# RWKV tiles: three factors moved into constants of small matrix products

## The chip, the cores and the metric

The kernel runs on one core of a Trainium2 chip. The metric is the device time of one execution, in microseconds (us). The kernel before took 769.58 us (median of three runs, 769.44 to 770.28). TensorE is written PE, VectorE DVE, ScalarE ACT, GpSimd POOL and the engine that issues most transfers SP.

## The reference, cut to what matters

One decoder layer: a norm and one input projection, then two groups of heads side by side (an RWKV-7 time mixing with 8 heads of 64, and a sparse attention), one output projection, and a gated feed-forward part. SEQ is 512 and D_MODEL 1024. The change touches the end of the RWKV group, where `y` is the result of the recurrence:

```python
    mean = jnp.mean(y, axis=-1, keepdims=True)
    var = jnp.mean(jnp.square(y - mean), axis=-1, keepdims=True)
    y = ((y - mean) * lax.rsqrt(var + LNX_EPS)).reshape(B, S, R_WIDTH) * lnx_w + lnx_b
    bonus = jnp.sum(rh * kh * r_k.astype(f32), axis=-1, keepdims=True) * vh
    y = (y + bonus.reshape(B, S, R_WIDTH)) * g
```

The recurrence is linear in `v`, so a `v` whose mean over each head's 64 channels has been taken away gives a `y` whose mean is zero; the kernel centres `v` and never centres `y`.

## The kernel before, in words

The program is written with a tile framework: a planner orders each engine's instructions at compile time by the program's order and by what is ready, and every buffer belongs to a tag with a fixed number of slots. A tile of a tag gets its slot at its first write, and waits for the release of an earlier tile when all slots are taken. So work of different parts runs interleaved on every engine.

The RWKV part keeps its tensors with channels on the partitions: `rar`, `rk_`, `rb`, `rv` are [128, 4, 512], where 128 partitions hold two heads (64 channels each), 4 is the pair of heads, and 512 the tokens. It works in four tiles of 128 tokens, each in three stages, in the order `stage_a(t)`, `stage_c(t-1)`, `stage_b(t)`, `bonus(t)`, with a `stage_c(3)` at the end:

- `stage_a` (L772) builds the tile's chunk matrices. L784 makes products of keys and queries, L787 masks them on DVE. Then four tensors are transposed to tokens on the partitions, four transposes each (L798). The second of them is `v`: DVE sums each head's 64 channels out of PSUM (L804) and two instructions, one for each half of the partitions, subtract the mean while they copy (L806). L813, L818, L826, L832, L838 and L843 are the products that follow.
- `stage_b` (L850) carries the state over the tile's two chunks (L862, L864, L865, L866).
- `bonus` (L876): four DVE instructions multiply r, the column `r_k` and k (L880), one product of 512 columns with `ones2` sums each head and spreads the sum over its channels (L882), DVE multiplies with `v` (L883), POOL adds `lnx_b` (L884).
- `stage_c` (L886): ACT squares `y` (L891), four products with 32 columns of `ones2` sum each head (L895), ACT copies the sums out (L896), a transpose puts tokens on the partitions (L897), DVE computes the inverse root in eleven small instructions (L899 and `rsqrt`, L449), ACT copies it 64 times for each head (L902), four transposes bring it back to channels (L904), and DVE multiplies it in (L906), multiplies by the weight `lnx_w` (L907), adds the bonus (L908) and multiplies by the gate (L909).

Beside these tiles PE, DVE, ACT and POOL run the attention (from L917 on: L980 and L981 scores, L986 to L990 softmax, L993 transposes of the probabilities, L1001 products with v, L965 and L969 the compressed branch). Before the tiles a triangular system is solved on DVE and POOL (`solve2`, L541, instructions L556 and L557; then `solve4`, L561). After them come the output projection and the feed-forward part (L163 to L165).

PSUM tag `rb` has one buffer, which `stage_b`, `bonus` and `stage_c` use in program order; `ra` has two, which `stage_a` uses. SBUF tag `t4` has four slots, which, among others, `cm` (constants and results of the compressed branch), `blk` and `inv` (the solve), `az` and `qt2` (the tiles), `gain2` (L1007) and three buffers of the feed-forward part's first weights (`t1`, `t3` and `t2`, loaded at L1123 and L1125, and written by DVE at L1141) take in turn. Tag `rp` has one slot, used in `compressed` (L684).

A product of two float32 operands is two MATMUL instructions in the trace; a transpose is one.

Of the kernel before, what the change touches and what calls it, by code (L numbers as in the profile page):

```python
# [12 lines left out]
AF = mybir.ActivationFunctionType  # L13
OP = mybir.AluOpType
AX = mybir.AxisListType
# [9 lines left out]
EPS, LNX_EPS = 1e-6, 64e-5  # L25
# [21 lines left out]
def hybrid_layer(ctx: ExitStack, tc: tile.TileContext, x, positions, norm_mix, w_in, mu_shift, w0, w2, a0, a2,  # L47
                 g2, k_k, k_a, r_k, lnx_w, lnx_b, pe_k, wk1, bk1, wk2, pe_v, wv1, bv1, wv2, w_out, norm_ffn,
                 w_gate, w_up, w_down, norm_final, out):
    nc = tc.nc  # L50
    PE, DVE, ACT, POOL = nc.tensor, nc.vector, nc.scalar, nc.gpsimd
# [6 lines left out]
    def ps(tag, shape=(128, 512), dtype=F32):  # L58
        return pp.tile(list(shape), dtype, name="ps_" + tag, tag=tag, bufs=PS_BUFS[tag])
# [3 lines left out]
    def st(shape, tag, bufs=1, dtype=F32):  # L63
        return sb.tile(list(shape), dtype, name=tag, tag=tag, bufs=SB_BUFS.get(tag, bufs))
# [17 lines left out]
    ident = st([128, 128], "ident")  # L82
# [38 lines left out]
    for g in range(2):  # L121
        nc.sync.dma_start(posci[g * 32:g * 32 + 31], bass.AP(tensor=positions.tensor, offset=positions.offset + 31,
                                                               ap=[[16, 31], [1, 1]]))
# [129 lines left out]
    ones2 = st([128, 128], "ones2")  # L253
# [9 lines left out]
    for c in range(2):  # L263
        h = amask[c * 64:(c + 1) * 64]
# [5 lines left out]
    for q in range(4):  # L270
        h = amaskd[32 * q:32 * q + 32]
# [38 lines left out]
    def col(name, i):  # L310
        return cs[:, row0[name] + i:row0[name] + i + 1]
# [57 lines left out]
    for a in range(2):  # L369
        p = ps("s", (128, 2, 256))  # L370
# [78 lines left out]
    def rsqrt(o, x):  # L449

        y, b = (st([128, 16], "rs", 3)[:, 0:x.shape[1]] for _ in range(2))
        DVE.tensor_scalar(b.bitcast(I32), x.bitcast(I32), 1, None, op0=OP.logical_shift_right)
        DVE.tensor_scalar(y.bitcast(I32), b.bitcast(I32), -1.0, 1597463007.0, op0=OP.mult, op1=OP.add)
        for n in range(3):
            DVE.tensor_mul(b, x, y)
            DVE.scalar_tensor_tensor(b, b, -0.5, y, op0=OP.mult, op1=OP.mult)
            DVE.scalar_tensor_tensor(o if n == 2 else y, b, 1.5, y, op0=OP.add, op1=OP.mult)
# [301 lines left out]
    uv = yuv[:, 1024:2048].rearrange("p (c h n) -> p c h n", c=2, h=8)  # L759
# [7 lines left out]
    pg = T["pg"]  # L767
    POOL.memset(ybd, 0.0)

    PQ = [(i, par, 2 * i + par, slice(par * 64, par * 64 + 64)) for i in range(4) for par in range(2)]  # L770

    def stage_a(t):  # L772
# [22 lines left out]
        for n, src in enumerate((rar[:, :, 0, tl], rv[:, :, tl], rb[:, :, tl], sk)):  # L795
            p = ps("ra", (128, 4, 128))
            for i in range(4):
                PE.transpose(p[:, i], src[:, i], ident)  # L798
            pv = p.rearrange("p i (q d) -> p (i q) d", q=2)
            if n == 0:  # L800
                ACT.activation(az[:, :, 0:64], pv, AF.Copy)
            elif n == 1:
                vs = st([128, 8], "vs", 2)
                DVE.tensor_reduce(vs, pv, axis=AX.X, op=OP.add)  # L804
                for c, cr, co in HALF:
                    DVE.scalar_tensor_tensor(uv[co, c], vs[cr, :, None].to_broadcast([64, 8, 64]), -1.0 / 64, pv[cr], op0=OP.mult, op1=OP.add)  # L806
            else:
                for c, cr, co in HALF:
                    ACT.activation(bk[cr if n == 2 else co, c], pv[cr], AF.Copy)
# [60 lines left out]
    def cb(name):  # L870
        return cs[:, row0[name]:row0[name] + 4, None].to_broadcast([128, 4, 128])

    def bonus_of(t):
        return abc[:, t, 4:8].rearrange("p h a s -> p h (a s)")

    def bonus(t):  # L876
        tl = slice(t * 128, t * 128 + 128)
        tmp = bonus_of(t)
        for i in range(4):
            DVE.scalar_tensor_tensor(tmp[:, i], rar[:, i, 1, tl], col("r_k", i), rk_[:, i, tl], op0=OP.mult, op1=OP.mult)  # L880
        p = ps("rb", (128, 4, 128))
        PE.matmul(p, ones2, tmp, start=True, stop=True)  # L882
        DVE.tensor_mul(tmp, p, rv[:, :, tl])  # L883
        POOL.tensor_add(tmp, tmp, cb("lnx_b"))  # L884

    def stage_c(t):  # L886

        tl = slice(t * 128, t * 128 + 128)
        ys = rar[:, :, 0, tl]
        tmp = abc[:, t, 0:4].rearrange("p h a s -> p h (a s)")  # L890
        ACT.activation(tmp, ys, AF.Square)  # L891

        p = ps("rb", (128, 2, 128))
        for i in range(4):
            PE.matmul(p[32 * i:32 * i + 32, 0], ones2[:, 48:80], tmp[:, i], start=True, stop=True)  # L895
        ACT.activation(tmp[:, 0], p[:, 0], AF.Copy)  # L896
        PE.transpose(p[:, 1], tmp[:, 0], ident)  # L897
        rn = st([128, 16], "rn", 2)[:, 0:8]
        DVE.tensor_scalar(rn, p[:, 1, 0:128:16], 1.0 / 64, LNX_EPS, op0=OP.mult, op1=OP.add)  # L899
        rsqrt(rn, rn)  # L900
        p = ps("rb", (128, 4, 128))
        ACT.activation(tmp.rearrange("p i (q d) -> p (i q) d", q=2), rn[:, :, None].to_broadcast([128, 8, 64]), AF.Copy)  # L902
        for i in range(4):
            PE.transpose(p[:, i], tmp[:, i], ident)  # L904
        yc = ys
        DVE.tensor_mul(yc, ys, p)  # L906
        DVE.tensor_mul(yc, yc, cb("lnx_w"))  # L907
        DVE.tensor_add(yc, yc, bonus_of(t))  # L908
        DVE.tensor_mul(yc, yc, gate_[:, :, tl])  # L909

# [352 lines left out]
```

## Time and profile before

| | |
|---|---|
| profiled execution | 770.73 us |
| its span (first to last instruction) | 769.0 us |
| mean granted TensorE clock | 0.984 of 2.4 GHz |
| PE busy | 738.6 us (96%), 6093 instructions |
| DVE busy | 543.3 us (71%), 1052 |
| ACT busy | 381.5 us (50%), 652 |
| POOL busy | 160.0 us (21%), 258 |
| chain of waits, by engine | PE 74%, DVE 15%, DMA 6% |

Busy time is the share of the span in which at least one instruction of the engine runs. Matmuls are pipelined, so one that lasts 270 ns may be followed 110 ns later by the next; what a run of them costs is read from the chain of waits, which gives each piece the time up to the next piece. The tiles run from about 213 to 350 us after the start of the span.

### The profile page before, as it was taken

How to read it: one execution, taken by the hardware profiler on the slowest of the kernel's cores; microseconds unless marked ns; L12 is line 12 of the kernel's file. 1: busy time of each engine (PE TensorE's matmuls, PEld its weight loads, DVE VectorE, ACT ScalarE, POOL GpSimd, SP SyncE). 2: the span in 40 equal slices, each digit the busy share in tenths (PEclk: the TensorE clock that was granted, in tenths of full speed). 3: DMA queues.
4: the chain of work that ended last, by engine and by line, in shares of the span. 5: the costliest groups of instructions: out<-in, count | busy, mean ns of one | idle time of the engine just before them, and what ended most of it. 6: DMA issues, size and time to landing. Idle time of an engine off the chain costs nothing.

```text
span 769.0 us, 14989 instructions
## 1 busy us (share of the span) xinstructions
PE 738.6 (96%) x6093; PEld 648.1 (84%) x6093; DVE 543.3 (71%) x1052; ACT 381.5 (50%) x652; POOL 160.0 (21%) x258
## 2 busy tenths in 40 slices
PE   8999999998889999999996899999999999999996
PEld 7867888898877878867786899999999998888885
DVE  5488689789768987875659497888695994333235
ACT  7398643224277776676447344444443552233224
POOL 3210054058345542442001102020202000000000
PEclk9999999999989999999998999999999999999998
DMA  7722543100051000321218569696768444322102
GB/s 247 223 82 84 164 110 110 55 2 2 3 219 30 3 1 3 85 83 56 83 55 192 110 176 203 161 223 151 161 159 221 112 153 147 110 68 97 55 1 110
DMA packets 69243, 82.83 MB, mean 108 GB/s; under 512 B 4868, under 2 KB 62806, under 8 KB 69174
## 3 DMA queue, kind: packets, MB, share of 16 engines
q1 hardware_dynamic: 57558, 70.34, 28.5%
q0 software_dynamic: 11616, 11.54, 9.9%
q8 instruction: 48, 0.79, 0.4%
q14 instruction: 21, 0.17, 0.1%
HBM read 79.77 MB, written 2.10 MB: 106 GB/s over the span
## 4 chain that ended last, share of the span: by engine, by line
PE 74%; DVE 15%; DMA 6%; issue 2%; ACT 1%; POOL 0%; SPq 0%; DVEq 0%; POOLq 0%; ACTq 0%
PE ps_ra L165 7%; PE ps_ra L164 7%; PE ps_ra L163 6%; PE ps_pj L165 6%; PE ps_pj L163 6%; PE ps_pj L164 6%; PE ps_s L165 4%; PE ps_s L163 4%; PE ps_s L164 4%; PE ps_o L1001 3%; DVE wlo L146 3%; PE ps_pj L993 2%; DMA L<-in_w_up_dram 2%; DMA wraw<-in_w_up_dram 2%; DMA L<-in_w_gate_dram 2%
## 5 line engine op out<-in xcount | busy, mean ns | idle before, releaser
L144 ACT ACTIVATE whi<-wraw 128x1024 fp32r<-128x1024 f32 (+1 forms) x79 | 78.5, 1033 | 33.2 <-PE ps_s L165 8.2
L146 DVE TENSOR_TENSOR wlo<-wraw,whi 128x1024 fp32r<-128x1024 f32 (+1 forms) x62 | 77.7, 1284 | 14.9 <-ACT whi L144 11.3
L146 DVE TENSOR_TENSOR L<-b,L 128x512 fp32r<-128x512 f32 x24 | 16.2, 691 | 57.1 <-PE ps_rb L164 55.1
L990 POOL TENSOR_SCALAR whi<-whi,m,gates 128x128 f32<-128x128 f32 (+3 forms) x64 | 42.5, 679 | 36.9 <-DVE m L988 28.7
L144 ACT ACTIVATE L<-b 128x512 fp32r<-128x512 f32 x24 | 14.9, 632 | 70.0 <-PE ps_rb L164 65.1
L164 PE MATMUL ps_ra<-wlo,L 128*128 128x256 f32 (+1 forms) x140 | 47.6, 340 | 0.2 <-DVE wlo L146 0.2
L163 PE MATMUL ps_ra<-whi,L 128*128 128x256 f32 (+1 forms) x140 | 47.4, 340 | 0.2 <-ACT L L144 0.2
L165 PE MATMUL ps_ra<-whi,L 128*128 128x256 f32 (+1 forms) x140 | 47.0, 337 | 0.0
L165 PE MATMUL ps_pj<-whi,L 128*128 128x256 f32 (+1 forms) x140 | 46.3, 332 | 0.0
L164 PE MATMUL ps_pj<-wlo,L 128*128 128x256 f32 (+1 forms) x140 | 46.3, 331 | 0.0
L163 PE MATMUL ps_pj<-whi,L 128*128 128x256 f32 (+1 forms) x140 | 45.9, 332 | 0.0
L164 PE MATMUL ps_ra<-L,whi 128*128 128x256 f32 (+2 forms) x128 | 44.3, 346 | 1.0 <-DVE L L146 1.0
L163 PE MATMUL ps_ra<-L,whi 128*128 128x256 f32 (+2 forms) x128 | 44.1, 345 | 0.9 <-ACT L L144 0.9
L165 PE MATMUL ps_ra<-L,wlo 128*128 128x512 f32 (+2 forms) x120 | 41.2, 343 | 0.0
L987 ACT ACTIVATE whi<-whi,m 128x128 f32<-128x128 f32 (+3 forms) x64 | 35.4, 554 | 9.3 <-DVE m L986 8.1
L165 PE MATMUL ps_pj<-L,wlo 128*128 128x512 f32 (+1 forms) x112 | 38.8, 346 | 0.1
L163 PE MATMUL ps_pj<-L,whi 128*128 128x512 f32 (+1 forms) x104 | 36.3, 349 | 0.2 <-ACT whi L144 0.2
L164 PE MATMUL ps_pj<-L,whi 128*128 128x512 f32 (+1 forms) x104 | 35.9, 346 | 0.0
L986 DVE CUSTOM_DVE_ANT_0 whi<-ps_s,negb 128x128 f32<-128x128 f32 (+3 forms) x64 | 29.3, 484 | 5.9 <-PE ps_pj L993 2.5
L1137 POOL DMA_DIRECT2D t<-in_w_up_dram x6 | 7.9, 1322 | 115.1 <-DVE whi L146 50.4
L163 PEld LDWEIGHTS ps_ra<-whi,L 128*128 128x128 f32 x140 | 27.6, 197 | 3.1 <-ACT L L144 0.6
L164 PEld LDWEIGHTS ps_ra<-wlo,L 128*128 128x128 f32 x140 | 27.5, 196 | 3.0 <-DVE wlo L146 0.5
(627 smaller groups left out, 2462.4 us busy)
## 6 DMA issues: line engine op xcount, KB each, us to landing
wraw<-in_w_gate_dram SPq DMA_DIRECT2D x22, 512.0 KB
wraw<-in_w_down_dram SPq DMA_DIRECT2D x11, 1024.0 KB
wraw<-in_w_in_dram SPq DMA_DIRECT2D x9, 1024.0 KB
t<-in_w_up_dram POOLq DMA_DIRECT2D x12, 512.0 KB, 7.4
wraw<-in_w_up_dram SPq DMA_DIRECT2D x11, 512.0 KB
L<-in_w_up_dram POOLq DMA_DIRECT2D x10, 512.0 KB, 8.9
wraw<-in_w_out_dram SPq DMA_DIRECT2D x4, 1024.0 KB
wraw<-in_w_in_dram SPq DMA_DIRECT2D x6, 512.0 KB
```

Source lines behind the costliest of these rows:

```text
L144: ACT.activation(hi, src, AF.Copy)
L146: (POOL if pool else DVE).tensor_sub(lo, src, hi.bitcast(F32))
L163: PE.matmul(o, lh, rh, start=start, stop=False)
L164: PE.matmul(o, lh, rl, start=False, stop=False)
L165: PE.matmul(o, ll, rh, start=False, stop=stop)
L986: DVE.tensor_tensor_reduce(pr[:, i], pS[:, i], negb[:, S - n:S], scale=-1.0, scalar=3e38, op0=OP.add, op1=OP.min, accum_out=m[:, i, 0:1])
L987: ACT.activation(pr[:, i], pr[:, i], AF.Exp, scale=-1.0, bias=m[:, i, 0:1], accum_out=m[:, i, 1:2])
L990: POOL.tensor_scalar(pr[:, i], pr[:, i], m[:, i, 2:3], gv[:, 1 + b0 + i, h:h + 1], op0=OP.mult, op1=OP.mult)
L993: PE.transpose(pT[:, j], prr[:, x, j * 128:j * 128 + 128], ident)
L1001: PE.matmul(po[q, 2 * g:2 * g + 2], vtok[:, j % (t + 1), b0 + j // (t + 1), g], pTs[:, par, j], start=False, stop=g == 1 and bs[-1] == 1 a ...
L1137: POOL.dma_start(t1, quarter(w_up, 0), accum_op=OP.add)
```

## The change

Constants are built once before the tiles. `onesr` is `ones2` scaled by the column `r_k`, one 128x128 block for each pair of heads (four POOL instructions). `lnxh` is the weight `lnx_w`, laid out as 8 rows (heads) by 4 blocks of 128 channels, loaded by one small transfer to 8 partitions and cut to each head's own 64 channels by two POOL selects. `heads` has a one where a channel belongs to a head. `centre` is the identity minus 1/64 in each head's block (one DVE instruction). `onesr` and `lnxh` live in a tile of tag `t4`, `heads` and `centre` in one of tag `rp`, both until the last tile.

In each tile, `v` is multiplied by `centre` in place of its transposes, so it arrives transposed and centred, and DVE only copies it. In `bonus` one DVE multiply over 512 columns replaces four over 128, and four products with `onesr` replace the one with `ones2`. In `stage_c` four products take the squares as the stationary operand and `heads` as 8 moving columns, and so give the sums with tokens on the partitions; the ACT copy and the transpose before the inverse root go. The inverse root (128x8) is transposed to 8x128, copied by ACT, and four products with `lnxh` spread it over the channels and apply the weight; the fourfold copy on ACT, the four transposes and DVE's multiply by `lnx_w` go.

```diff
     POOL.memset(ybd, 0.0)
 
+    con = st([128, 2, 4, 128], "t4")
+    onesr, lnxh = con[:, 0], con[0:8, 1]
+    for i in range(4):
+        POOL.tensor_scalar(onesr[:, i], ones2, col("r_k", i), None, op0=OP.mult)
+    nc.sync.dma_start(lnxh, bass.AP(tensor=lnx_w.tensor, offset=lnx_w.offset, ap=[[0, 8], [128, 4], [1, 128]]))
+    POOL.affine_select(lnxh, lnxh, pattern=[[128, 4], [1, 128]], compare_op=OP.is_ge, fill=0.0, base=0, channel_multiplier=-64)
+    POOL.affine_select(lnxh, lnxh, pattern=[[-128, 4], [-1, 128]], compare_op=OP.is_ge, fill=0.0, base=63, channel_multiplier=64)
+    con2 = st([128, 2, 4, 32], "rp").rearrange("p a b c -> p (a b c)")
+    heads, centre = con2[:, 0:32].rearrange("p (i h) -> p i h", h=8), con2[:, 32:160]
+    POOL.memset(heads, 0.0)
+    for q in range(2):
+        v = con2[q * 64:q * 64 + 64, q:q + 1]
+        POOL.memset(bass.AP(tensor=v.tensor, offset=v.offset, ap=[list(v.ap[0]), [10, 4]]), 1.0)
+    DVE.scalar_tensor_tensor(centre, ones2, -1.0 / 64, ident, op0=OP.mult, op1=OP.add)
...
             for i in range(4):
-                PE.transpose(p[:, i], src[:, i], ident)
+                if n == 1:
+                    PE.matmul(p[:, i], src[:, i], centre, start=True, stop=True)
+                else:
+                    PE.transpose(p[:, i], src[:, i], ident)
...
             elif n == 1:
-                vs = st([128, 8], "vs", 2)
-                DVE.tensor_reduce(vs, pv, axis=AX.X, op=OP.add)
                 for c, cr, co in HALF:
-                    DVE.scalar_tensor_tensor(uv[co, c], vs[cr, :, None].to_broadcast([64, 8, 64]), -1.0 / 64, pv[cr], op0=OP.mult, op1=OP.add)
+                    DVE.tensor_copy(uv[co, c], pv[cr])
...
         tmp = bonus_of(t)
+        DVE.tensor_mul(tmp, rar[:, :, 1, tl], rk_[:, :, tl])
+        p = ps("rb", (128, 4, 128))
         for i in range(4):
-            DVE.scalar_tensor_tensor(tmp[:, i], rar[:, i, 1, tl], col("r_k", i), rk_[:, i, tl], op0=OP.mult, op1=OP.mult)
-        p = ps("rb", (128, 4, 128))
-        PE.matmul(p, ones2, tmp, start=True, stop=True)
+            PE.matmul(p[:, i], onesr[:, i], tmp[:, i], start=True, stop=True)
...
         p = ps("rb", (128, 2, 128))
         for i in range(4):
-            PE.matmul(p[32 * i:32 * i + 32, 0], ones2[:, 48:80], tmp[:, i], start=True, stop=True)
-        ACT.activation(tmp[:, 0], p[:, 0], AF.Copy)
-        PE.transpose(p[:, 1], tmp[:, 0], ident)
+            PE.matmul(p[:, 0, 0:8], tmp[:, i], heads[:, i], start=i == 0, stop=i == 3)
         rn = st([128, 16], "rn", 2)[:, 0:8]
-        DVE.tensor_scalar(rn, p[:, 1, 0:128:16], 1.0 / 64, LNX_EPS, op0=OP.mult, op1=OP.add)
+        DVE.tensor_scalar(rn, p[:, 0, 0:8], 1.0 / 64, LNX_EPS, op0=OP.mult, op1=OP.add)
         rsqrt(rn, rn)
+        PE.transpose(p[0:8, 1], rn, ident)
+        rnT = tmp[0:8, 0]
+        ACT.activation(rnT, p[0:8, 1], AF.Copy)
         p = ps("rb", (128, 4, 128))
-        ACT.activation(tmp.rearrange("p i (q d) -> p (i q) d", q=2), rn[:, :, None].to_broadcast([128, 8, 64]), AF.Copy)
         for i in range(4):
-            PE.transpose(p[:, i], tmp[:, i], ident)
+            PE.matmul(p[:, i], lnxh[:, i], rnT, start=True, stop=True)
         yc = ys
         DVE.tensor_mul(yc, ys, p)
-        DVE.tensor_mul(yc, yc, cb("lnx_w"))
```

## Rows read from the trace of the kernel before

**Rows 1.** Busy time of each engine in five stretches from the middle of the tiles to the end of the output projection (us from the span's start; in each column the busy time and the number of instructions, then PE's granted clock, the DMA engines' busy share and GB/s).

```profile
265.00:290.00 25.00, 25.00 (x302) 19.95 (x300) 21.08 (x73) 17.89 (x47) 12.37 (x20) 1.00 0.01 2
290.00:315.00 25.00, 24.77 (x342) 19.79 (x336) 20.18 (x62) 15.37 (x38) 6.86 (x10) 1.00 0.08 23
315.00:333.00 18.00, 18.00 (x237) 13.53 (x233) 15.71 (x44) 10.85 (x25) 9.01 (x9) 1.00 0.52 148
333.00:352.00 19.00, 18.11 (x126) 12.74 (x125) 15.43 (x53) 14.34 (x36) 9.97 (x12) 1.00 0.00 1
352.00:399.00 47.00, 47.00 (x227) 37.10 (x227) 25.04 (x36) 21.17 (x33) 2.26 (x3) 1.00 0.25 79
```

**Rows 2.** What PE waited for from 226 to 352 us (total us, times, longest), the largest of the five rows.

```profile
PE ps_pj L965 <- DVE t L962: 0.9, 1, 0.9
PE ps_ra L798 <- DVE whi L787: 0.2, 1, 0.2
PE ps_rb L882 <- DVE L L866: 0.2, 1, 0.2
...
```

**Rows 3.** Pieces of the chain of waits (start, us until the next piece, what): eight products of 128x128x128 in float32; then the products and transposes that the change replaces.

```profile
250.74 1.79 PE ps_ra L818 x16
...
271.29 0.86 PE ps_rb L882 x2
...
276.90 0.36 PE ps_rb L895 x8
...
279.68 0.26 PE ps_rb L897
...
344.89 0.44 PE ps_rb L904 x4
```

**Rows 4.** PE's timeline: eight products with a 128x128 float32 tile as the stationary operand and two moving columns.

```profile
130.60 1.95 PE L476 MATMUL ps_s<-ones,L 128*128 128x2 f32 x16
```

**Rows 5.** The chain of waits at the start of tile 0.

```profile
213.57 2.55 DVE L L880 x4
216.14 0.68 DVE whi L787
...
219.13 0.70 DVE whi L787
...
219.88 1.12 PE ps_ra L798 x4
```

**Rows 6.** Busy times as in rows 1, in three stretches of tile 0.

```profile
218.00:220.00 2.00, 0.72 (x8) 0.58 (x7) 1.92 (x6) 1.39 (x3) 0.19 (x1) 0.67 1.02 420
220.00:222.00 2.00, 2.00 (x13) 2.00 (x13) 1.61 (x3) 0.92 (x3) 1.26 (x2) 0.50 0.99 306
...
224.00:226.00 2.00, 2.00 (x35) 1.69 (x34) 0.00 (x0) 1.85 (x4) 1.05 (x1) 0.62 0.95 384
```

**Rows 7.** DVE's instructions of the lines that the change touches and of two that are like the new ones (duration in ns: least, median, most; then first and last start in us).

```profile
L804 DVE TENSOR_REDUCE vs<-ps_ra x4: 679/680/691, 221.0 to 301.3; 128x8 f32<-128x512 f32 x4
L806 DVE SCALAR_TENSOR_TENSOR wlo<-vs,ps_ra x8: 680/686/690, 221.8 to 303.2; 64x512 f32<-64x512 f32 x8
L880 DVE SCALAR_TENSOR_TENSOR L<-L,cs,b x16: 343/347/815, 213.6 to 292.3; 128x128 f32<-128x128 f32 x16
L907 DVE TENSOR_TENSOR L<-L,cs x4: 682/686/691, 262.0 to 347.5; 128x512 f32<-128x512 f32 x4
L908 DVE TENSOR_TENSOR L<-L x4: 684/684/965, 264.1 to 348.8; 128x512 f32<-128x512 f32 x4
L580 DVE COPY L<-ps_s x4: 678/684/689, 210.7 to 212.8; 32x512 f32<-32x512 f32 x4
```

**Rows 8.** Two steps of the solve on DVE, from its timeline (start, us, instruction).

```profile
192.69 0.35 DVE L557 TENSOR_TENSOR t<-t,smask 128x120 f32<-128x120 f32 x1
...
195.22 1.11 DVE L557 TENSOR_TENSOR t<-t,smask 128x105 f32<-128x105 f32 x1
```

**Rows 9.** The first multiply into `qt2` and the first step of the solve on POOL (the idle time before it in brackets), and the last products that read `cm`.

```profile
131.68 1.15 POOL L794 TENSOR_TENSOR t<-b,dend 128x512 f32<-128x512 f32 x1
...
161.58 1.23 POOL L556 TENSOR_TENSOR smask<-t,t 128x31 f32<-128x31 f32 x1 [28.66 <-DVE rot L239]
...
L698 PE MATMUL ps_s<-t,rp x8: 217/274/275, 160.4 to 165.2; 128*128 128x64 f32 x8
```

**Rows 10.** The loads of `t1` and `t3` on SP's queue, POOL's transfer that adds to `t3`, and the first DVE instruction that reads `t1`.

```profile
214.12 0.42 SPq L1123 DMA_DIRECT2D t<-in_w_gate_dram  x1
...
310.52 0.37 SPq L1125 DMA_DIRECT2D t<-in_w_up_dram  x1
...
315.00 1.33 POOL L1138 DMA_DIRECT2D t<-in_w_up_dram  x1 [3.83 <-DMA t<-in_w_up_dram]
...
L1141 DVE TENSOR_TENSOR t<-t,wraw x6: 1224/1226/1226, 379.5 to 610.5; 128x1024 f32<-128x1024 f32 x6
```

**Rows 11.** ACT's two instructions of `stage_c` that go.

```profile
L896 ACT ACTIVATE L<-ps_rb x4: 267/277/277, 245.2 to 334.2; 128x128 f32<-128x128 f32 x4
...
L902 ACT ACTIVATE L<-rn x4: 612/621/631, 257.1 to 342.6; 128x512 f32<-128x512 f32 x4
```

**Rows 12.** The chain of waits between tiles 2 and 3: the first and the last of a run of pieces on DVE, with the PE piece that follows it.

```profile
291.02 0.42 DVE b L846
...
298.50 0.70 DVE whi L787
...
299.34 0.63 PE ps_ra L798 x4
```

## The prediction

> **What bounds the kernel now.** I read the page's shares first: PE is busy for 96% of the span and holds 74% of the chain of waits, DVE 71% and 15%. Since the change touches only the RWKV tiles, I then read that stage by stretches [rows 1]. The reader is to see that PE is busy for 25.00 of 25, 24.77 of 25, 18.00 of 18 and 18.11 of 19 us, at full clock, and for 47.00 of 47 us in the output projection behind the tiles, while DVE is at 15.4 to 21.1 us and has room. Busy PE time is modelled, so the list of PE's waits was the check [rows 2]: from 226 to 352 us the largest wait is 0.9 us, and with the two rows left out, of 0.2 us each, all five sum to 1.7 us. PE never runs dry there because the attention fills it. So from 226 us on, a microsecond more on PE is a microsecond more in the end, and a microsecond less on DVE is worth at most its part of 1.7 us.
>
> Tile 0 is different. Its start hangs on DVE: after the solve DVE runs the four L880 of the bonus in 2.55 us, then the masks, and PE's transposes follow at 219.88 [rows 5]. PE is busy for 0.72 of 2 us before that, and its granted clock falls to half (1.2 GHz) until some way into 224 to 226 us [rows 6].
>
> **The change part by part, PE.** The price of a float32 product: sixteen instructions of L818, eight products of 128x128x128, take 1.79 us [rows 3], so an instruction is 0.112 us and four products (eight instructions) 0.90 us. Four transposes take 0.44 us (L904, the same shape as L798) [rows 3].
> - Centring: four transposes become four such products, +0.46 us. Three tiles at full clock give 1.4; in tile 0 L798 takes 1.12 us at half clock [rows 5], so I double its addition to 0.9. Together +2.3.
> - Bonus: L882's one product of 512 columns takes 0.86 us [rows 3], four of 128 columns 0.90: +0.04 a tile, +0.15.
> - Sums of the squares: L895's eight instructions take 0.36 us in all [rows 3], because each fills only 32 columns of the array. The new products load a whole 128x128 tile and move 8 columns. The nearest row is L476, the same stationary tile with 2 columns: sixteen instructions in 1.95 us, of which the last one's drain is some 0.25, so 0.11 each [rows 4]. Eight make 0.90: +0.54 a tile, +2.15. The low end is L895's own rate, +0. The transpose L897 (0.26) goes and the one of the inverse root comes, which I put at the same.
> - Spreading with the weight: four transposes of 0.44 become four products with 8 rows and 128 moving columns. I take 0.90, L818's, for the columns are as many: +0.46 a tile, +1.85. The low end is L895's rate, 0.36, which would be a gain of 0.1 a tile, -0.3.
>
> The sum on PE is +6.4 us, with +2.1 as the low end. The Trainium skill, "TensorE: Matmul & The Clock Gate", section "Back-to-back issue gap", puts an isolated matmul of 1 to 64 columns at a floor of about 25 ns; by that the eight instructions with 8 columns would cost 0.2 us a tile, and the sum would be 2.8 us lower. L476's rate in rows 4 speaks against it: there the load of the stationary tile sets the pace.
>
> **DVE, ACT and POOL.** A tile loses L804 (0.68), L907 (0.69) and the difference between four L880 and one multiply like L908 (about 1.14 against 0.69 at their median durations, starts overlapping); L806 becomes a copy out of PSUM of the same length, by L580 [rows 7]. That is 1.8 us a tile, 7.3 in all, and ACT loses 0.62 and 0.28 for a new copy of about 0.27 [rows 11]. From tile 1 on nearly all of it falls where PE is the bound: I take -0.3 us, from 0 to -1.7 [rows 2]. In tile 0 it is on the path: the 2.55 us of L880 (the longest took 815 ns, against 347 in the median) were run beside POOL's instructions, so the one multiply costs 0.69 undisturbed and perhaps 1.5 disturbed, by the same ratio. I take -1.1, from -0.4 to -1.9.
>
> The constants: four scalings, two selects, three clears on POOL, one small transfer, and the instruction for `centre` on DVE, about 0.35 us by L880's median. POOL stands idle for 28.66 us before the solve [rows 9], which hides its share; without that cover it would be some 3 us of POOL beside the solve. `con` is first written ahead of `qt2` in the program, so it takes the slot of `t4` that L794 took at 131.68; L794 then has to wait for `cm`, read until 165.2 [rows 9], and runs beside the solve or behind it. There a step of the solve on DVE takes 1.11 us where a longer one took 0.35 [rows 8], when POOL multiplies at the same time: +0.75. `centre` waits for the slot of `rp`, which `compressed` frees at about 170, inside the solve as well: +0.35. Together +1.1, from 0 to +1.5.
>
> The slot that `con` keeps has one more result: `t1`'s load (214.12) finds no slot and waits for `az`, as `t3`'s does now (310.52). Nobody reads it before 379.5 us [rows 10], so I cost the delay at nothing. But POOL's transfers that add to `t1` and `t3` wait in POOL's queue for these loads (3.83 us for `t3`), and behind them stand L990, L961 and L884, for which PE's attention products wait. The one that comes new into 310 to 335 us costs between 0 and 3.8; I take 0, since PE had other work while POOL stood in the first.
>
> **The sum.** 6.4 - 1.1 - 0.3 + 1.1 = +6.1 us. The profiled execution took 770.73 us (span 769.0 and 1.7 around it), and would take 776.8; it lies 1.15 above the median of 769.58, from which I forecast 775.7. The ends: all lows give -1.5 (2.1 - 1.9 - 1.7, the constants at nothing), all highs +11.3 (6.4 - 0.4 + 1.5 + 3.8).
>
> **Rivals.**
> 1. DVE ends last in the tiles, and the new products run in PE's gaps. For it: the chain of waits runs over DVE from 291.02 to 299.2 between tiles 2 and 3 [rows 12], and over L880 in tile 0. Against it: PE is busy for 24.77 of 25 us around that very stretch [rows 1]; it had other work. If true, DVE's 7.3 us less the 1.1 come off: 763.4. It decides as soon as PE's waits in the tiles are more than the added 6 us; they are 1.7. Chance 0.12.
> 2. The clock stays up in tile 0. PE's thin stretch before 219.88 gets shorter by 1.1 us or more, and the half clock around it may not come. That lasts about 6.8 us: a mean of 0.67 over two us is 1.3 us at half and the rest at full clock, 0.62 is 1.5 us, and the four us between them are taken whole [rows 6]. It costs half of this, 3.4 us, and centring's 0.46 extra: 6.1 - 3.9 = +2.2, 771.8. Against it: PE stays thin for over 3 us there whatever the bonus costs. The Trainium skill says on the same page, in Part 4 on PE-mode transpose, that transposes do not count as a busy PE for the clock; four of those in this stretch become products, which by that rule would bring the clock back sooner. No row here tells transposes and products apart in this. Chance 0.11.
> 3. POOL's transfer for `t1` holds up the attention by its whole wait: +9.9, 779.5. For it: POOL is busy for 9.97 of 19 us in the last tile [rows 1], and PE's one long wait (L965) is in a chain with POOL. Against it: PE lost nothing visible at the first such wait. Chance 0.10.
> 4. The small products are cheap (the low ends of both): +1.8, 771.4. Against it stands L476. Chance 0.05.
>
> **How the numbers follow.** The forecast, +3 to +9 us, gets 0.62. 770.5 to 780.0 holds it, rival 2, rival 3 and half of rival 4, and leaves out rival 1 and the tails. What a measurement tells from no change is about 0.2%, 1.5 us. Faster by more than that is rival 1, 0.12; within it, half of rival 4 and the low parts of rival 2 and of the forecast, 0.08; slower 0.80.
>
> **What would show it.** Right: PE busy for all but a few tenths of each stretch from 226 us to the end of the output projection, the centring products at 0.90 us for eight instructions and the sums at the same, and DVE's busy time down by some 6 to 7 us with no gain from it; `t1`'s load near 310 us. Wrong: PE's list of waits in the tiles grown by several us (then another engine or the one `rb` buffer has become the bound), the eight instructions with 8 columns in 0.4 us or less, the first transposes of tile 0 earlier by much more than 1 us, or an end of the output projection that has not moved although PE's work has grown.

## The result and the profile after

The changed kernel takes 781.19 us (median of 4 runs, 779.88 to 782.26); the ratio to the kernel before is 1.0144, with a 95% interval from 1.0124 to 1.0164, so it is about 11 us slower. Forecast were 775.7, in a range from 770.5 to 780.0. The profiled execution has a span of 780.6 us against 769.0.

Line numbers of the new kernel are higher by 14 to 18 in the tiles (L798 becomes L816 and, for `v`, L814; L818 becomes L834; L895 becomes L910; L904 becomes L919); in the solve they are the same. The first thing to read is where the 11.65 us between the two spans arise. These are starts and ends of the same instructions in both traces (us from the span's start):

| | before | after | later by |
|---|---|---|---|
| last small product before the solve (L529 ends) | 158.67 | 159.61 | 0.9 |
| POOL's first step of the solve (L556 starts) | 161.58 | 164.62 | 3.0 |
| POOL's last step (L557 ends) | 194.77 | 206.93 | 12.2 |
| DVE turns the solution (L563 starts) | 201.04 | 207.30 | 6.3 |
| the solve's products (L578 ends) | 211.63 | 221.36 | 9.7 |
| first L813, tile 0 | 224.24 | 227.17 | 2.9 |
| last L843, tile 3 | 323.32 | 328.72 | 5.4 |
| attention's last product (L1001 ends) | 367.29 | 383.01 | 15.7 |
| last transposes of the second norm (L1082 end) | 418.49 | 433.94 | 15.4 |
| last product of all (starts) | 761.76 | 773.41 | 11.65 |

Three readings. The solve, which the change does not touch, ends 6 to 12 us later. The last L843 of the tiles comes only 5.4 us later, the attention's end 15.7: in PE's queue the attention fills what the tiles leave, so whatever PE loses shows at the attention's end. And the feed-forward part gives 4 us back.

Busy times by stretch, in the columns of [rows 1], for the new kernel:

```profile
226.00:250.00 24.00, 21.07 (x311) 18.93 (x309) 12.57 (x37) 16.19 (x41) 7.79 (x13) 0.93 0.01 3
250.00:275.00 25.00, 24.00 (x357) 19.79 (x358) 19.27 (x72) 14.64 (x45) 9.42 (x20) 1.00 0.01 2
275.00:300.00 25.00, 24.27 (x330) 20.50 (x329) 18.73 (x71) 19.13 (x55) 13.05 (x22) 1.00 0.01 2
300.00:325.00 25.00, 25.00 (x318) 21.01 (x315) 21.48 (x66) 14.66 (x35) 9.27 (x12) 1.00 0.20 42
355.00:400.00 45.00, 44.75 (x237) 32.82 (x236) 24.41 (x49) 24.80 (x45) 8.39 (x11) 1.00 0.19 59
```

PE is still the bound from 250 us on, but no longer in the first tile (21.07 of 24 us, at a granted clock of 0.93). Its waits from 226 to 360 us, as in [rows 2], now sum to 5.0 us in nine rows, of which the four largest are:

```profile
PE ps_s L947 <- ACT L L948: 1.2, 1, 1.2
PE ps_ra L834 <- ACT t L830: 0.9, 1, 0.9
PE ps_ra L829 <- ACT wraw L825: 0.8, 1, 0.8
PE ps_pj L1007 <- ACT wraw L1011: 0.7, 1, 0.7
...
```

The prices of the new products, as pieces of the chain at full clock, beside [rows 3]: centring (L814), bonus (L898), sums (L910), the transpose of the inverse root (L914), spreading with the weight (L919), and the unchanged L834 as a measure.

```profile
274.15 0.89 PE ps_ra L814 x8
275.04 0.89 PE ps_rb L898 x8
283.21 1.78 PE ps_ra L834 x16
286.56 0.11 PE ps_rb L914
288.72 1.08 PE ps_rb L919 x8
310.44 0.79 PE ps_rb L910 x8
```

Centring costs 0.45 more than four transposes, the bonus 0.03 more than its one product, the sums 0.43 more than L895, the spreading 0.64 more than L904, and the transpose of the inverse root 0.15 less than L897. That is 1.40 us a tile, 5.6 in four, against 6.4 forecast, of which 0.46 was for tile 0 at half clock.

Counted from the end of the last L529, the attention ends 14.8 us later. PE's waits of 0.2 us and more up to there sum to 13.2 us against 9.4 before, and 6.8 us more at half clock (13.6 against 6.8) are worth up to 3.4; with the products these make 12.8, and 2 us are left without a row. So the larger part of the 14.8 is not the products, and begins ahead of the tiles. POOL's queue at the start of the solve (start, us, instruction, idle time before it in brackets), and one line from further on:

```profile
164.51 0.15 POOL L711 MEMSET rot<- 128x64 f32 x1 [22.07 <-DVE kct L240]
164.62 0.24 POOL L556 TENSOR_TENSOR smask<-t,t 128x31 f32<-128x31 f32 x1
164.81 1.65 POOL L776 TENSOR_SCALAR_AFFINE_SELECT t<-t 8x512 f32<-8x512 f32 x1
166.44 0.27 POOL L557 TENSOR_TENSOR t<-t,smask 128x31 f32<-128x31 f32 x1
166.79 0.34 POOL L556 TENSOR_TENSOR smask<-t,t 128x60 f32<-128x60 f32 x1
167.09 1.05 POOL L809 TENSOR_TENSOR t<-b,dend 128x512 f32<-128x512 f32 x1
...
193.78 0.96 POOL L768 MEMSET wlo<- 128x1024 f32 x1 [4.75 <-PE ps_ra L164]
```

A memset (L711) that waits for DVE now stands ahead of the solve; before, it stood behind POOL's second step. A select and the displaced multiply (L809, before: L794) lie between the first steps. The memset of `ybd` (L768) waits 4.75 us for PE, and POOL's steps of the solve wait behind it; before, it came five steps later in the solve and waited 0.18 us. All four multiplies of L808 (L793 before) come inside POOL's part of the solve; before, three of them came behind its last step. PE in turn was slow there: it waited 2.8 us at 183.8 for the copy L623 (1.7 before), and its granted clock fell:

```profile
186.00:193.00 7.00, 6.33 (x33) 6.34 (x34) 6.60 (x17) 2.29 (x5) 2.49 (x8) 0.52 0.00 1
213.00:216.00 3.00, 3.00 (x159) 2.79 (x154) 2.81 (x5) 2.93 (x7) 2.37 (x4) 1.00 0.88 299
216.00:219.00 3.00, 0.38 (x23) 0.26 (x16) 2.30 (x4) 0.12 (x1) 0.00 (x0) 1.00 1.03 415
```

The last two lines show another loss. PE's timeline across the solve's products:

```profile
212.20 2.21 PE L572 MATMUL ps_s<-t,L 32*32 32x32 f32 x128
214.34 1.10 PE L799 MATMUL ps_ra<-L,b 64*64 64x128 f32 x30
215.37 1.00 PE L578 MATMUL ps_s<-L,t 32*32 32x32 f32 x50
219.44 1.92 PE L578 MATMUL ps_s<-L,t 32*32 32x32 f32 x78 [3.07 <-issue]
```

After 50 of L578's 128 products PE stands still for 3.07 us with no releaser, while the DMA engines are wholly busy (1.03). In the kernel before, 22 projection products lay between L572 and L578, L578 ran through in 2.2 us, and the transfers began only behind it.

### The profile page after: what moved, and what is told of

Read it like the earlier page. It is cut to its first block, busy times and chain, and to the rows that moved or that the text cites. A ratio compares the mean times of both kernels' runs of the same rounds, so it can differ in the third digit from the quotient of the medians.

```text
span 780.6 us, 15092 instructions
## 1 busy us (share of the span) xinstructions
PE 747.0 (96%) x6149; PEld 658.8 (84%) x6149; DVE 542.5 (70%) x1033; ACT 379.2 (49%) x648; POOL 162.8 (21%) x267
## 4 chain that ended last, share of the span: by engine, by line
PE 86%; DVE 9%; ACT 2%; issue 1%; DMA 1%; SPq 0%; DVEq 0%; ACTq 0%
PE ps_ra L164 8%; PE ps_ra L165 8%; PE ps_ra L163 8%; PE ps_pj L165 7%; PE ps_pj L163 7%; PE ps_pj L164 7%; PE ps_s L163 5%; PE ps_s L164 5%; PE ps_s L165 5%; PE ps_o L1015 3%; PE ps_pj L1007 2%; DVE wlo L146 2%; PE ps_s L994 1%; PE ps_ra L834 1%; PE ps_s L995 1%
## 5 line engine op out<-in xcount | busy, mean ns | idle before, releaser
L146 DVE TENSOR_TENSOR wlo<-wraw,whi 128x1024 fp32r<-128x1024 f32 (+1 forms) x62 | 77.1, 1273 | 15.4 <-ACT whi L144 11.5
L163 PE MATMUL ps_ra<-whi,L 128*128 128x256 f32 (+1 forms) x140 | 48.6, 348 | 0.4 <-ACT L L144 0.4
L165 PE MATMUL ps_ra<-whi,L 128*128 128x256 f32 (+1 forms) x140 | 48.2, 344 | 0.0
L1001 ACT ACTIVATE whi<-whi,m 128x128 f32<-128x128 f32 (+3 forms) x64 | 35.4, 555 | 8.9 <-DVE m L1000 8.7
```

The lines of the kernel that those rows point to most:

```text
L146: (POOL if pool else DVE).tensor_sub(lo, src, hi.bitcast(F32))
L163: PE.matmul(o, lh, rh, start=start, stop=False)
L165: PE.matmul(o, ll, rh, start=False, stop=stop)
L1001: ACT.activation(pr[:, i], pr[:, i], AF.Exp, scale=-1.0, bias=m[:, i, 0:1], accum_out=m[:, i, 1:2])
```

## The experiments

Differences in us are the ratio to the kernel before times its median, with the 95% interval in brackets. Two parts of one change rarely add exactly here, since the planner orders every kernel anew. One such order, far behind the tiles, is worth about 4 us by itself; it is found below, at e9_centre_bonus, and kernels that differ in it have to be compared with care.

**The constants without the tiles, and the tiles without the constants.** First the change's block of constants in the kernel before, used by nobody.

> The kernel before with the constants built exactly as in the change, and used by nobody; the tiles keep their old instructions. Theory A (the constants disturb the solve: POOL's part of it ends some 12 us later, PE idles there and falls to half clock, and PE never gets this back): slower by 3 to 6 us, with POOL's last step of the solve near 205 us instead of 194.6 and a second stretch of half clock between 180 and 240 us. Theory B (all of the loss is the products in the tiles, and the late solve is covered by PE's other work): within 1 us of before. Theory C (the slot that the constants keep delays a weight load and through it the attention): within 1 us of before, for here the slot is given back at once.

Measured: +5.5 (3.7 to 7.2). The kept trace, of its shortest execution (771.56 us), has POOL's last step of the solve end at 203.91. Counted from the last L529, the attention ends 6.2 us later than before and the second norm's last transposes 4.7. Up to the attention's end half clock takes as long as before (6.8 us), and PE's waits sum to 15.3 us against 9.4: in this execution the loss is waiting. Then the other half:

```diff
+    heads = st([128, 16], "heads")        # at the program's start, tags of their own
+    centre = st([128, 128], "centre")
...
     def bonus(t):
+        if t == 0:
+            constants()                   # onesr and lnxh in t4, behind stage_a(0)
```

> The whole change in the tiles, but the constants away from the solve: the two small ones in tiles of their own at the start of the program, the two large ones built behind the first stage of tile 0. Theory A: slower than before by the price of the products alone, 5 to 8 us, with the solve's instructions on POOL in the order and at the times of before. Theory B: slower by 10 to 12 us, as the change. Theory C: slower by 10 to 12 us, for the large constants keep their slot through all tiles.

Measured: +6.7 (4.6 to 8.8), with POOL's solve from 161.55 to 194.78, within 0.03 us of before. The two halves sum to 12.2 where the change costs 11.1, within the intervals: theory A holds, B and C fall. C falls in the change's own trace too: `t1`'s load went at 315.76, as forecast, and PE's list of waits shows no wait that follows from it.

**The bonus alone.**

```diff
-            DVE.scalar_tensor_tensor(tmp[:, i], rar[:, i, 1, tl], col("r_k", i), ...)
+        DVE.tensor_mul(tmp, rar[:, :, 1, tl], rk_[:, :, tl])
...
-        PE.matmul(p, ones2, tmp, start=True, stop=True)
+            PE.matmul(p[:, i], T["onesr"][:, i], tmp[:, i], start=True, stop=True)
```

> The kernel before with the bonus of the change alone (one multiply on DVE, four products with scaled blocks), its one constant built behind the first stage of tile 0. By the prediction's own terms -1.1 us at the start of tile 0 and +0.15 on PE: faster by about 1 us. If the four scalings on POOL stand in the way in tile 0, or if PE's clock drops elsewhere: slower by 1 to 3 us.

Measured: -0.9 (-2.2 to 0.3). The size is that of the forecast, but it is not told apart from nothing.

**The gap of 3 us.** A one-element write into each buffer, which reads the solve's result, holds the transfers back.

```diff
+    def hold(v):
+        with tc.high_priority():
+            DVE.tensor_copy(v, T["abc"][0:1, 2, 0, 0, 32:33])
+    hold(x2[0:1, 0, 0:1])
     nc.sync.dma_start(x2, ...)
```

> The constants alone, as in e1_constants, and the loads that follow the last projection (x, the second norm's weight, the first piece of w_out, the first weights of the feed-forward part) held back until the solve's second step has been copied out of PSUM, by a one-element write into each of their buffers. PE's order up to the last tile is that of e1_constants. Theory D (PE's 3.1 us without any visible release inside L578 is its own instructions arriving late, because the transfers fill the DMA engines at that moment): the gap shrinks to under 1 us, the half clock behind it goes or moves, and the time is 2 to 5 us under e1_constants, so 771 to 774 us. Rival (256 small products in a row outrun the fetch whatever else is being moved): the gap stays at 3 us and the time within 1 us of e1_constants.

> The change with the same loads held back in the same way. Theory D: the gap of 3.1 us inside L578 goes and the time falls by 2 to 5 us, to 776 to 779 us. Rival: no change, 780 to 782 us. If the first weights of the output projection then come too late, PE waits at its start near 370 us and the gain is lost.

Measured: +6.5 (4.4 to 8.7) and +10.2 (8.6 to 11.8). The element that is read is written once more by tile 2's squares, so the transfers were held to 313 us in the change, longer than meant. The gap is gone; PE's timeline of the change with held transfers (its lines are numbered 4 higher), and two of its stretches:

```profile
214.18 1.00 PE L582 MATMUL ps_s<-L,t 32*32 32x32 f32 x50
215.40 1.45 PE L582 MATMUL ps_s<-L,t 32*32 32x32 f32 x78 [0.22 <-issue]
```

```profile
213.00:216.00 3.00, 2.78 (x131) 2.45 (x127) 2.89 (x5) 1.88 (x4) 1.18 (x2) 1.00 0.02 5
216.00:217.00 1.00, 1.00 (x55) 0.96 (x49) 0.99 (x2) 0.00 (x0) 0.00 (x0) 1.00 0.00 0
```

So the transfers make the gap: 0.22 us in place of 3.07, with the same products in the same order. But the time does not fall by 2 to 5 us; both kernels agree with their partners within the intervals. Counted from the same product before the solve, the held change reaches the end of the attention 3.0 us sooner and loses this in the feed-forward part, where PE waits 2.3 us that the change did not. The held constants reach it 2.2 us later than e1_constants, as other waits come in the gap's place. Theory D is right on the cause of the gap; what the gap is worth stays open.

**Which constant.** The four scaled blocks alone, then the weight's load and selects alone, each written as in the change and read by nobody.

> The kernel before with one of the constants alone: the four scaled blocks in the tile of tag t4, used by nobody. L794's first multiply loses its slot as in the change, and the memset L711 stands ahead of the solve on POOL; there is no small load and no select. If the displaced multiply or the memset starts the delay of the solve: slower by 3 to 6 us, as e1_constants. If the two selects do: within 1 us of before.

> The kernel before with another of the constants alone: the weight's small load and its two selects in the tile of tag t4, used by nobody. L794's first multiply loses its slot as well, and the selects stand around the solve's first step on POOL; the memset L711 stays behind it. If the displaced multiply starts the delay: slower by 3 to 6 us. If the memset does: within 1 us of before. If the selects do: slower by 3 to 6 us here and no change in e6_ones.

Measured: +4.5 (3.0 to 6.2) and +1.1 (-0.3 to 2.5). The selects are not it. In e7_ln the displaced multiply lies behind POOL's first step of the solve; in e6_ones it lies ahead of that step, behind the memset L711. Is it the slot?

```diff
+    con = st([128, 2, 4, 128], "t4")
+    POOL.memset(con[0:1, 0, 0, 0:1], 0.0)
```

> The kernel before with nothing but an empty tile of tag t4, of which one element is cleared, at the place where the change writes its first constant. Every engine's order is that of before except for L794's first multiply, which loses its slot and stands ahead of POOL's first step of the solve, waiting for the last reader of cm. If that displaced multiply is what costs in e6_ones: POOL's solve starts 3 to 4 us later, and the kernel is slower by 3 to 5 us. If what costs there is PE's order (all projections ahead of the solve's products) and not the multiply: POOL's solve still starts 3 to 4 us later, but the kernel is within 1.5 us of before.

Measured: -0.9 (-1.8 to 0.0). This run didn't put the question as meant: an unread tile gives its slot back at once, so the multiply waited for nothing and ran early.

```profile
132.87 2.10 POOL L796 TENSOR_TENSOR t<-b,dend 128x512 f32<-128x512 f32 x1
161.02 1.34 POOL L556 TENSOR_TENSOR smask<-t,t 128x31 f32<-128x31 f32 x1 [26.05 <-DVE rot L239]
```

It shows that another place for that multiply in the queue costs nothing as long as it waits for nothing.

**PE's queue, then POOL's.** Counted from the last L524, 66 projection products stand ahead of L572 in the change, 67 in e6_ones, 34 in the kernel before. Of the 291 behind the last L529 this leaves none in the change, 7 in e6_ones and 33 in the kernel before for later, beside and behind the solve's products. The next kernel puts all of them ahead and leaves POOL's solve as it was, by tracing `solve4` one job later:

```diff
-then((cols(RCOLS), job_qs(0)), solve3, solve4), (cols(RCOLS + 256), job_qs(1))]
+then((cols(RCOLS), job_qs(0)), solve3), then((cols(RCOLS + 256), job_qs(1)), solve4)]
```

> The kernel before with the solve's last step traced behind the last projection: every order up to there is that of before (POOL's solve too, and there are no constants), but PE has all 67 remaining projection products ahead of L572, as in the change (66 there, 34 in the kernel before), and none left beside L572 and L578. Theory E (what costs in e1_constants and e6_ones is this place in PE's queue: the projections that filled PE's waits behind L572 are used up, the transfers that follow them start early, and PE idles in tile 0): slower by 2 to 5 us, with a gap of up to 3 us inside L578. Rival (what costs is POOL's late solve; the place in the queue only follows from it): within 1.5 us of before.

Measured: +1.2 (0.4 to 2.1). The gap is there, without any constant:

```profile
PE ps_s L578 <- issue: 3.3, 1, 3.3
```

The +1.2 alone would speak for the rival. But e11_order differs in the feed-forward part as well, in the order that is worth about 4 us (below): DVE's split stands ahead of the add there, and in the kernel before behind it.

```profile
433.33 1.23 DVE L146 TENSOR_TENSOR whi<-t,whi 128x1024 fp32r<-128x1024 f32 x1 [0.40 <-ACT whi L144]
438.22 1.23 DVE L1141 TENSOR_TENSOR L<-L,wraw 128x1024 f32<-128x1024 f32 x1 [3.66 <-DMA L<-in_w_up_dram]
```

Up to the second norm, ahead of that order, its trace is 3.7 us later than before (counted from the last L529), and against e15_swap, which is the kernel before with the same order, it is 5.2 us slower. So the place in PE's queue costs 4 to 5 us, about as theory E has it. e7_ln is the counterpart: POOL's solve ends 4.0 us later in it, 32 projection products are left for later, one fewer than before, the feed-forward order is that of before, and it costs 1.1. That speaks for PE's queue too, but not cleanly, for e7_ln's kept trace (773.10 us, against its median of 771.18) is as late at the second norm as e11_order's. Last, e6_ones with the memset taken from the solve's front:

```diff
-        kcA0 = st([128, 64], "rot", 2)
+        kcA0 = st([128, 64], "kcz")
```

> e6_ones with the memset L711 in a tile of its own, so that it no longer stands ahead of POOL's solve and L794's first multiply runs long before it. POOL's solve starts as in the kernel before; the memset L768 and L793's multiplies, which wait for PE, still stand inside it, and 70 projection products ahead of L572. If the late start is the cause of e6_ones: within 1.5 us of before (e11_order had the same place of L572 and lost 1.2). If what stands inside the solve is: POOL's solve still ends near 200 us, and the kernel is slower by 3 to 5 us.

Measured: +3.6 (2.3 to 4.9). POOL starts the solve at 161.53, as before, and ends it at 204.78. Its waits from 158 to 213 us (total us, times, longest):

```profile
POOL b L797 <- PE ps_s L524: 4.6, 4, 2.7
POOL wlo L768 <- PE ps_ra L164: 3.1, 1, 3.1
```

L797 is the old L793, a multiply for the tiles; as in the change, all four lie inside the solve, and each waits for PE. PE for its part is at half clock for most of the time in between; the same stretch before has 1.00 in the clock's column.

```profile
187.00:205.00 18.00, 18.00 (x178) 16.06 (x178) 13.46 (x43) 4.27 (x8) 10.27 (x25) 0.53 0.01 2
```

The memset was not it: the split stands ahead of the add in this kernel and behind it in e6_ones, so the times can't be set side by side, but up to the second norm both traces are late by the same (4.9 and 4.7 us). What both share is the place in PE's queue (8 and 7 products left for later), which by e11_order alone costs 4 to 5 us, and tile work on POOL inside the solve. What the tile work and the clock add to the first is not shown; no run has the one without the other.

**The tiles' parts.** Centring and bonus without the new `stage_c`:

> e2_late without its part in stage_c: the centring products and the new bonus alone, their constants away from the solve, the norm's spread and weight as before. By the prediction's terms: centring +2.3, bonus +0.15, start of tile 0 -1.1, together about +1.3 us, so 770.5 to 772.5 us, and the products of stage_c (+4.0) would be the difference to e2_late. If stage_c costs nothing: 5 to 7 us slower, as e2_late. If centring on PE pays off in tile 0: faster than e3_bonus, below 769 us.

Measured: -1.2 (-2.1 to -0.2), better than forecast, and 7.9 below e2_late, twice the price of `stage_c`'s products. The cause lies far behind the tiles: the feed-forward part holds a wait of 0 to 3.6 us that comes and goes with the kernel. In the kernel before it is DVE's queue: an add waits for its transfer, behind it stands the split for which PE waits.

```profile
430.30 0.69 DVE L1191 TENSOR_TENSOR t<-ps_s,t 128x512 f32<-128x512 f32 x1 [5.10 <-PE ps_s L165]
436.08 1.23 DVE L1141 TENSOR_TENSOR L<-L,wraw 128x1024 f32<-128x1024 f32 x1 [5.09 <-DMA L<-in_w_up_dram]
437.22 1.22 DVE L146 TENSOR_TENSOR whi<-t,whi 128x1024 fp32r<-128x1024 f32 x1
```

```profile
PE ps_pj L165 <- DVE whi L146: 2.5, 1, 2.5
```

In the changed kernel the planner happened to put the split first; that is where it gets back most of its 4 us. e9_centre_bonus has it first as well, and e2_late has not:

```profile
434.00 1.23 DVE L146 TENSOR_TENSOR whi<-t,whi 128x1024 fp32r<-128x1024 f32 x1 [0.40 <-ACT whi L144]
438.62 1.23 DVE L1152 TENSOR_TENSOR L<-L,wraw 128x1024 f32<-128x1024 f32 x1 [3.39 <-DMA L<-in_w_up_dram]
```

Putting it first by hand:

```diff
+            if q == 1:
+                with tc.issue_after(last[0].ins):     # the first weights' last split
+                    DVE.tensor_add(t2, t1, b22)
```

> e3_bonus, and in the feed-forward part the one DVE add that waits for a transfer (L1141, 5 us) queued behind the last split of the first weights, for which PE waits 2.5 us in the kernel before at 436 us. No other order changes up to there. If the wait is DVE's queue, as read from the trace: it goes, and the time is 2 to 4 us under e3_bonus, 765 to 768 us. If the split itself waits for its transfer or its buffer: no change against e3_bonus.

Measured: -5.4 (-6.9 to -4.0), 764.31 us. DVE's queue in this kernel:

```profile
428.23 0.69 DVE L1202 TENSOR_TENSOR t<-ps_s,t 128x512 f32<-128x512 f32 x1 [5.44 <-PE ps_s L165]
429.32 1.23 DVE L146 TENSOR_TENSOR whi<-t,whi 128x1024 fp32r<-128x1024 f32 x1 [0.40 <-ACT whi L144]
433.33 1.23 DVE L1150 TENSOR_TENSOR L<-L,wraw 128x1024 f32<-128x1024 f32 x1 [2.78 <-DMA L<-in_w_up_dram]
```

> The kernel before with nothing but DVE's waiting add queued behind the last split of the first feed-forward weights. If the wait of 2.5 us on PE at 436 us is worth its length and half of the half clock behind it: faster by 2 to 4 us. If most of what e10_best gained is the bonus, let through by this: faster by 1 us or less.

> e10_best once more, beside e15_swap on one chip: 764 to 767 us, 2 to 4 us under e15_swap if the bonus adds what its profile shows at the end of the attention (2.9 us).

Measured: -4.0 (-5.5 to -2.5) and -4.8 (-6.3 to -3.2). The order is worth most of it; the bonus adds 0.8, as it did alone, and not the 2 to 4 that were expected. This version beats both kernels.

By the traces the planner put the split first in the change, e1_constants, e4_hold_const, e9_centre_bonus, e11_order and e17_ones_kcz, and the add first in the kernel before, e2_late, e3_bonus, e5_hold_change, e6_ones, e7_ln and e8_slot. So the times of the first group hold a gain of about 4 us that has nothing to do with what they change: 4.0 by e15_swap, and two more pairs, e13_late_swap with e2_late and e10_best with e3_bonus, give 3.2 and 4.5. Against e15_swap, its partner in this order, the change costs 15.1, the constants of e1_constants 9.5, e17_ones_kcz 7.6 and e11_order 5.2 (each to about 2 us).

Now the tiles' parts once more, all in one order: e14_heads is e10_best with the new sums of squares, e12_centre_swap is e9_centre_bonus with the order made sure by hand, e13_late_swap is e2_late with the new order.

> e10_best with one half of the new stage_c: the sums of squares by four products with the heads as 8 moving columns; the inverse root is copied, transposed and weighted as before. Eight instructions of 0.11 us in place of L895's 0.36 and L897's 0.26 a tile: +0.25 a tile, +1.0 in all, so 764.5 to 766.5 us. If the stationary load of whole tiles stalls PE more: 3 us or more.

> e9_centre_bonus with DVE's waiting add queued as in e10_best. If centring on PE is worth what e9_centre_bonus and e3_bonus show together (no difference within 1.5 us): 763 to 766 us, as e10_best. If the prediction's price holds (+2.3 on PE): 2 us above e10_best.

> e2_late with the same add queued as in e10_best, so that the feed-forward part takes nothing back: e12_centre_swap plus the two new products of stage_c. If these cost what their instructions take (+4.2 us on PE): 767 to 770 us. If stage_c costs the 8 us that lie between e9_centre_bonus and e2_late: 771 to 774 us, and then the longer way through PE and the one buffer of rb, not the products, is the larger half.

Measured: -4.2 (-5.2 to -3.2), 0.1 (-0.9 to 1.1) and 3.5 (2.2 to 4.8). The sums cost 1.2 over e10_best (forecast by their instructions: 1.0), the whole of `stage_c` 3.4 over e12_centre_swap (4.2), and centring 5.5 over e10_best. That e9_centre_bonus had cost nothing over e3_bonus is the order: e9_centre_bonus already had it, so e12_centre_swap is nearly the same kernel, and against e10_best e9_centre_bonus costs 4.2. Centring so costs 4.2 to 5.5 where 2.3 was forecast. The traces put the end of the second norm 3.2 us later in e12_centre_swap than in e10_best, 1.8 of it the four tiles' products at 0.45; where the rest comes from stays open.

## Why the prediction was wrong

**The step that failed** is the term for the constants: "Together +1.1, from 0 to +1.5." It measured 5.5 in e1_constants, wholly outside the bounds. With the feed-forward order equal it is more: 9.5 there, and 7.6 in the change, which is e13_late_swap (+3.5) with the constants ahead of the solve. What was named did happen: L794 fell into the solve, beside DVE's steps. I counted what is added to POOL (its own time) and to DVE (a longer step), but not what the planner moves with it. POOL is not free beside the solve: it does 62 of its 112 instructions (L556 and L557), in its own queue, in order; a memset went ahead of them and tile work that waits for PE went in between. And in PE's queue the projection products that used to fill the waits beside and behind the solve's products went ahead of these, which costs 4 to 5 us without any constant (e11_order). How the rest divides between POOL's queue and PE's clock is not shown. The sentence that POOL's 28.66 idle us "hide" the scalings [rows 9] is true for their 3.83 us and misses their effect on all that is ordered after them.

**PE's products** were priced well: +6.4 forecast, with tile 0 at half clock; 5.6 at full clock, as read above. The low columns were priced by L476's rate [rows 4] and came out at 0.79 us for eight instructions, 0.10 each. The Trainium skill, "TensorE: Matmul & The Clock Gate", section "Back-to-back issue gap", says beside its floor for single products that in a stream of loads and products both set the spacing; the trace agrees with that sentence, and by the floor alone eight would have taken 0.2. The spreading was the worst term: 1.08, where 0.90 was taken. Rival 4 falls.

**The tiles as a whole**, -1.1, -0.3 and +6.4, were to cost 5.0; without the constants they cost 6.7 (4.6 to 8.8), and 7.5 in the order of e13_late_swap against e15_swap. The part that was priced too low is centring, 4.2 to 5.5 against 2.3. That PE is the bound there, so that DVE's savings are worth next to nothing, held: rival 1 falls. PE's waits in the tiles did grow, from 1.7 to 5.0 us. DVE's busy time went down by 0.8 us over the span and not by 6 to 7, because others grew, among them L239: its eighteen instructions took 7.1 us against 4.7, beside POOL's shifted work.

**Tile 0**: the forecast of -1.1 fits e3_bonus (-0.9), but in the change it drowns in the late solve. Rival 2 falls in the change: the half clock comes at 220.1 and again at 230.3, for 6.8 us together, as long as before. That it can stay away, the kept traces of e10_best and e12_centre_swap show, with full clock through tile 0. Rival 3 falls: POOL's transfer for `t1` waited 3.25 us, PE for nothing behind it.

**The range** ended at 780.0, with a sum of all highs of 11.3 above the start; the result lies at that sum by luck, with other terms than those that were to reach it. In one order of the feed-forward part the constants cost 7.6 and the tiles 7.5, and the planner's order gave 4.0 back, which nobody had forecast: 11.1.

## What to carry to other kernels

Where a planner writes the order, price a new instruction by the queue it enters, and by everything the planner will order anew around it: here constants that no tile read cost 5.5 us, because the planner moved other work into half of a solve that ran on a seemingly idle engine, and the solve's products to another place in PE's queue. Build constants where the engine's next long chain is over, and check in the trace that the chain starts and ends where it did, with the same work around it on every engine. Before trusting a difference of a few microseconds, look downstream for a wait that comes and goes, such as an instruction that waits for a transfer ahead of one that another engine needs; taking this one out gained 4 us by itself, and while it differed between the runs it hid the price of two causes, centring and PE's queue.

## What the runs showed of the hardware

A run of small products can starve while transfers fill the DMA engines: gaps of 3.07, 3.12 and 3.32 us in the change, e1_constants and e11_order, 0.22 us where the transfers were held back. The list of transfers has packets of 16 KB in a queue of the kind "instruction"; in the change one at 216.9 us falls into the gap, the first since 204.5, and PE had gone through some 540 instructions in between, where the same stretch of the kernel before has about 310 and 280 between packets, and the change with held transfers 380 and 320. The 0.79 MB of that queue come to 64 bytes for each of PE's 12,298 instructions and loads. That PE waited for its own instructions is inferred from this; that the transfers cause the wait is shown.
